# Sixteen starting places for the weight forms of the gate pairs and couples of a bidirectional trunk layer

## The chip, the cores and the metric

The kernel runs on one core of one Trainium2 chip, whose engines appear in the profile as PE (TensorE matmuls), PEld (TensorE weight loads, which overlap the matmuls), DVE (VectorE), ACT (ScalarE), POOL (GpSimd) and SP (SyncE, which issues most DMAs). The metric is the device time of one execution in microseconds, the median over several executions. A shorter time is better.

## The reference

One layer of an encoder on 512 positions of width 1024, all in float32. Only the matrix products matter here:

```python
proj = rmsnorm(x, g_pre_mix) @ w_in                  # q k v g u sv a_ret a_sgu
y_ret = (layernorm(retention(q, k, v)) * silu(g)) @ w_ret_o
y_sgu = (gelu(u) * spatial(layernorm(gelu(sv)))) @ w_sgu_o
x1 = x + rmsnorm((sigmoid(a_ret) * y_ret + sigmoid(a_sgu) * y_sgu) @ w_out, g_post_mix)
hid = conv3(rmsnorm(x1, g_pre_ffn) @ w_up)           # width 2 * 2816
y = x1 + rmsnorm((gelu(hid_a) * hid_b) @ w_down, g_post_ffn)
```

## The kernel before

**Precision.** Every float32 operand is split into a high and a low part of a faster float32 form (`split`, lines 83 to 85: ACT copies the high part, DVE subtracts it from the source and leaves the low part). A product is then three matmuls, high by high, high by low and low by high, accumulated in PSUM.

**Seven products for eight.** For some pairs of weight blocks the kernel doesn't use the weights as they are but seven sums of their quarters, called forms: B11, B21, T1, T2, T3, T4 and B22 (`FORMS`, line 91). `w_form` (lines 152 to 170) loads a pair of weight blocks, makes the sums on DVE and POOL, and splits each form into a tile `wf`: 512 columns of high part, then 512 columns of low part. `Pair` (from line 646) multiplies them. Its `product` (line 655) is twelve matmuls on line 662, four steps of three: the stationary operand is a slice of 128 columns of `wf`, the moving operand 256 columns of an activation (`xh` and `xl`, `h2h` and `h2l`) or of an activation form (`sh`, `sl`). A pair thus has 7 times 12, or 84 matmuls on line 662.

**Which pairs.** There are twenty: four for the column u of `w_in` (list places 32 to 39), eight for the gates a_ret and a_sgu (list places 40, 44, ... 68; `GATE0` is 40, `GATE1` is 72), and eight couples of the up projection (`COUPLES`, list places `UP0 + 2 * a` for a = 4, 6, ... 18, where `UP0` is 80). In a gate pair and in a couple the forms alternate with two whole weight blocks of 8 times three matmuls with 512 moving columns (`f_block`, lines 212 to 214).

**Where weights lie.** All weights of this kind come from one ring of nine slots (`slot`, lines 122 and 123). A slot has 1088 float32 elements, 4352 bytes or 17 times 256, so all nine start at the same place modulo 256 bytes. An argument `at` shifts the tile inside its slot by a number of elements: whole blocks start at 0 (at 48 in the down projection, line 138), weight forms at 16 (line 168), the weights of the down projection's own forms at 48 (line 188). A shift of 16 elements is 64 bytes. The activations are in blocks of 2048 bytes, and in the program their ring starts at the same place modulo 256 bytes as the ring of slots; a half of such a block (columns 256 to 511) starts 1024 bytes further, which is the same place again. So the distance modulo 256 bytes between the start of a stationary slice and the start of the moving operand is the tile's shift: 0 bytes for whole blocks, 64 bytes for forms. In the down projection the weights are the moving operand, at 192 bytes, and the activations the stationary one, at 0: 64 bytes again, counted in the same direction.

**Order.** Loads, splits and forms are issued ahead of their use by `w_get` (line 198), which keeps a fixed number of units in flight (`LOOK` is 4). The order on each engine is that of the program text. ACT, DVE and POOL prepare weights and activations while PE multiplies.

Of the kernel before, what the change touches and what calls it, by code (L numbers as in the profile page):

```python
# [27 lines left out]
U0, GATE0, GATE1 = 32, 40, 72  # L28
# [8 lines left out]
UP0 = DOWN0 - 2 * NF  # L37
COUPLES = [(i, i + 1) for i in range(4, 20, 2)]
# [8 lines left out]
def tile_block(ctx: ExitStack, tc, xT, x, wall, par, cs, wsp, bsp, gpost, gffn, out):  # L47
# [7 lines left out]
    def nm(s):  # L55
        uid[0] += 1
        return f"{s}_{uid[0]}"
# [25 lines left out]
    def split(hi, lo, src):  # L83
        copy(hi, src)
        nc.vector.tensor_sub(lo, src, as32(hi))  # L85
# [7 lines left out]
    i = 0  # L93
    while i < NW:
# [7 lines left out]
        elif i == UP0 + 2 * COUPLES[0][0]:  # L102
# [3 lines left out]
            i = UP0 + 2 * COUPLES[-1][1] + 2  # L106
# [12 lines left out]
    def raw_tile():  # L119
        return sb.tile([P, 1024], F32, tag="raw", bufs=4, name=nm("raw"))  # L120

    def slot(n, at=0, w=1024):
        return sb.tile([P, 1088], F32R, tag="w4", bufs=9, name=nm(n))[:, at : at + w]

    def w_block(i):
# [23 lines left out]
                split(hi, lo, raw)  # L149
        return hi, lo  # L150

    def w_form(form, i):

        if form == "B11":
            a, b = raw_tile(), raw_tile()
            nc.sync.dma_start(a, wall[i])
            nc.sync.dma_start(b, wall[i + 1])
            w_raw["B11"], w_raw["B12"] = a[:, :S], a[:, S:]
            w_raw["B22"], w_raw["B21"] = b[:, :S], b[:, S:]
        elif form == "T1":  # L160
            t = raw_tile()
            w_raw["T1"], w_raw["T2"], w_raw["T3"], w_raw["T4"] = t[:, :S], t[:, S:], w_raw["B12"], t[:, S:]
            nc.vector.tensor_add(w_raw["T1"], w_raw["B11"], w_raw["B12"])  # L163
            nc.vector.tensor_add(w_raw["T3"], w_raw["B12"], w_raw["B22"])
            nc.gpsimd.tensor_tensor(out=w_raw["T2"], in0=w_raw["T1"], in1=w_raw["B22"], op=ALU.add)  # L165
        elif form == "T4":
            nc.gpsimd.tensor_tensor(out=w_raw["T4"], in0=w_raw["T2"], in1=w_raw["B21"], op=ALU.add)
        w = slot("wf", 16)
        split(w[:, :S], w[:, S:], w_raw[form])
        return w[:, :S], w[:, S:]  # L170

# [20 lines left out]
    def w_unit(u):  # L192
        return w_block(u[1]) if u[0] == "blk" else (w_down if u[0] in "qt" else w_form)(*u)
# [4 lines left out]
    def w_get(look=LOOK):  # L198

        i = w_pos[0]  # L200
        w_pos[0] += 1
        room = 2 * look + (2 if w_size(units[i]) == 2 else 0)
        n = sum(w_size(u) for u in units[i : w_pos[1]])
        while w_pos[1] < len(units) and (w_pos[1] <= i or n + w_size(units[w_pos[1]]) <= max(room, 9 if look == LOOK else 0)):
            u = units[w_pos[1]]
            w_ready[w_pos[1]] = w_unit(u)
            w_pos[1] += 1
            n += w_size(u)
        return w_ready.pop(i)
# [768 lines left out]
    i = 0  # L978
# [83 lines left out]
    for j in range(DP):  # L1062
# [5 lines left out]
        if j in (3, 5):  # L1068
            w = w_get()
# [179 lines left out]
```

## Time and profile before

| | |
|---|---|
| median of three runs | 840.68 us (840.61 to 841.0) |
| the profiled execution | 839.4 us, of which the span of the profile is 837.6 us |
| mean granted TensorE clock | 0.994 |
| PE busy, instructions | 820.8 us (98%), 5152 |
| PEld busy | 738.7 us (88%) |
| DVE busy | 663.0 us (79%) |
| ACT busy | 429.7 us (51%) |
| POOL busy | 109.9 us (13%) |

The profile lists busy times by engine, a view of the span in slices, the chain of work that ended last, and groups of instructions by source line and by tiles. In a row such as `L662 PE MATMUL ps<-sh,wf` the tile written stands before the arrow and the tiles read behind it, with the buffer numbers left out. The end of a matmul is modelled, so the time of a single one overlaps the next; what it really takes in a stream is the distance between two starts. The view of the chain in order of time gives the start of a stretch, its length and, behind an x, how many instructions it merges.

### The profile page before, as it was taken

The numbers are of one execution on the slowest core, as the hardware profiler recorded it, in microseconds if no ns is written. First come the engines' busy times: TensorE is split into PE (matmuls) and PEld (weight loads), VectorE is DVE, ScalarE is ACT, GpSimd is POOL, SyncE is SP. The second block draws the span as 40 slices with busy tenths as digits, with TensorE's granted clock in tenths as the row PEclk, the third lists the DMA queues.
The fourth block names the chain that finished last, engine by engine and source line by source line (L and its number), as shares of the span: only waits on it lengthen the run. The fifth ranks groups of instructions, "written<-read, shape, count | busy, mean of one in ns | idle before, by whom it ended". The sixth has DMA issues, their size and how long they took to land.

```text
span 837.6 us, 13230 instructions
## 1 busy us (share of the span) xinstructions
PE 820.8 (98%) x5152; PEld 738.7 (88%) x5152; DVE 663.0 (79%) x1100; ACT 429.7 (51%) x729; POOL 109.9 (13%) x110
## 2 busy tenths in 40 slices
PE   9999999999999999999999999899999999999995
PEld 7888888888899999999988898799999998999995
DVE  7489888877897776877665669779799799988956
ACT  6635446545664533444444654456566566544531
POOL 0010000111221111122211224111111100000001
PEclk9999999999999999999999999999999999999998
DMA  8733212212233333333457120333333341233334
GB/s 286 246 114 111 76 66 76 75 51 101 88 101 102 101 101 101 101 99 103 136 161 283 65 63 26 101 101 101 101 101 101 101 151 51 76 117 123 114 126 152
DMA packets 29215, 93.24 MB, mean 111 GB/s; under 512 B 3360, under 2 KB 4000, under 8 KB 29152
## 3 DMA queue, kind: packets, MB, share of 16 engines
q1 hardware_dynamic: 26928, 86.85, 31.7%
q0 software_dynamic: 1360, 4.46, 1.6%
q10 hardware_dynamic: 864, 1.09, 0.4%
q8 instruction: 40, 0.66, 0.3%
q14 instruction: 23, 0.19, 0.1%
HBM read 88.19 MB, written 4.19 MB: 110 GB/s over the span
## 4 chain that ended last, share of the span: by engine, by line
PE 84%; DVE 10%; issue 2%; DMA 2%; ACT 1%; POOL 0%; DVEq 0%; POOLq 0%; ACTq 0%
PE ps L662 20%; PE ps L212 11%; PE ps L213 11%; PE ps L214 11%; PE ps L1017 6%; PE ps L473 5%; PE ps L474 5%; PE ps L475 5%; DVE wf L85 2%; PE ps L810 2%; PE ps L812 2%; PE ps L811 2%; DMA raw<-wall 2%; DVE dl L85 1%; PE ps L1033 1%
## 5 line engine op out<-in xcount | busy, mean ns | idle before, releaser
L85 DVE TENSOR_TENSOR wl<-raw,wh 128x1024 fp32r<-128x1024 f32 (+1 forms) x93 | 108.0, 1171 | 53.2 <-PE ps L662 29.1
L78 ACT ACTIVATE wf<-raw 128x512 fp32r<-128x512 f32 x140 | 84.4, 625 | 94.9 <-PE ps L213 45.8
L85 DVE TENSOR_TENSOR wf<-raw,wf 128x512 fp32r<-128x512 f32 x140 | 107.8, 785 | 26.9 <-ACT wf L78 25.9
L662 PE MATMUL ps<-sh,wf 128*128 128x256 f32 x640 | 123.3, 282 | 2.2 <-ACT sh L78 1.7
L78 ACT ACTIVATE wh<-raw 128x1024 fp32r<-128x1024 f32 (+2 forms) x95 | 93.1, 989 | 35.6 <-DMA raw<-wall 16.1
L662 PEld LDWEIGHTS ps<-sh,wf 128*128 128x128 f32 x640 | 102.2, 188 | 3.7 <-ACT sh L78 1.9
L212 PE MATMUL ps<-h2h,wh 128*128 128x512 f32 (+1 forms) x256 | 93.2, 366 | 0.0
L213 PE MATMUL ps<-h2l,wh 128*128 128x512 f32 (+1 forms) x256 | 93.2, 365 | 0.0
L214 PE MATMUL ps<-h2h,wl 128*128 128x512 f32 (+1 forms) x256 | 92.8, 363 | 0.0
L662 PE MATMUL ps<-sl,wf 128*128 128x256 f32 x320 | 90.0, 281 | 1.5 <-DVE sl L85 1.5
L473 PE MATMUL ps<-wh,xh 128*128 128x512 f32 x192 | 75.0, 391 | 0.0
L474 PE MATMUL ps<-wl,xh 128*128 128x512 f32 x192 | 74.9, 390 | 0.0
L475 PE MATMUL ps<-wh,xl 128*128 128x512 f32 x192 | 74.8, 390 | 0.0
L165 POOL TENSOR_TENSOR raw<-raw,raw 128x512 f32<-128x512 f32 x20 | 34.3, 1716 | 223.0 <-DVE raw L163 166.5
L662 PEld LDWEIGHTS ps<-sl,wf 128*128 128x128 f32 x320 | 61.3, 192 | 2.3 <-DVE sl L85 1.7
L1017 PE MATMUL ps<-dh,fh 128*128 128x256 f32 x216 | 60.1, 278 | 1.6 <-DVE e L1051 1.2
L1017 PE MATMUL ps<-dl,fh 128*128 128x256 f32 x216 | 60.0, 278 | 0.1
L1017 PE MATMUL ps<-dh,fl 128*128 128x256 f32 x216 | 59.9, 277 | 0.0
L214 PEld LDWEIGHTS ps<-h2h,wl 128*128 128x128 f32 x256 | 48.5, 190 | 7.8
L212 PEld LDWEIGHTS ps<-h2h,wh 128*128 128x128 f32 x256 | 48.4, 190 | 7.3 <-ACT h2h L878 0.3
L662 PE MATMUL ps<-xh,wf 128*128 128x256 f32 x288 | 54.7, 281 | 0.0
L213 PEld LDWEIGHTS ps<-h2l,wh 128*128 128x128 f32 x256 | 48.6, 190 | 6.6
(303 smaller groups left out, 2053.2 us busy)
## 6 DMA issues: line engine op xcount, KB each, us to landing
raw<-wall SPq DMA_DIRECT2D x145, 512.0 KB, 3.6
x<-x SPq DMA_DIRECT2D x24, 256.0 KB, 5.7
xT<-xT SPq DMA_DIRECT2D x8, 256.0 KB, 5.4
x<-x POOLq DMA_DIRECT2D x8, 256.0 KB, 2.3
xT<-xT POOLq DMA_DIRECT2D x4, 256.0 KB, 4.0
out<-zg SPq DMA_DIRECT2D x4, 256.0 KB, 2.1
out<-zs ACTq DMA_DIRECT2D x3, 256.0 KB, 3.8
cs<-cs SPq DMA_DIRECT2D x2, 256.0 KB, 4.2
```

The costliest lines, as they stand in the source:

```text
L78: nc.scalar.activation(out=o, in_=i, func=AF.Copy)
L85: nc.vector.tensor_sub(lo, src, as32(hi))
L165: nc.gpsimd.tensor_tensor(out=w_raw["T2"], in0=w_raw["T1"], in1=w_raw["B22"], op=ALU.add)
L212: nc.tensor.matmul(o, ah, bh, start=start, stop=False)
L213: nc.tensor.matmul(o, ah, bl, start=False, stop=False)
L214: nc.tensor.matmul(o, al, bh, start=False, stop=stop)
L473: nc.tensor.matmul(acc[t], xh[k][:, c], wh[:, f], start=k == 0, stop=False)
L474: nc.tensor.matmul(acc[t], xh[k][:, c], wl[:, f], start=False, stop=False)
L475: nc.tensor.matmul(acc[t], xl[k][:, c], wh[:, f], start=False, stop=k == KD - 1)
L662: nc.tensor.matmul(o, w_[:, c], a_, start=first and k == n == 0, stop=k == 3 and n == 2, skip_group_check=True,)
L810: nc.tensor.matmul(o, ah, bh, start=k == 0, stop=False)
L1017: nc.tensor.matmul(o, a_[:, c], w_[:, f], start=j == t == i == 0, stop=j == DP - 1 and i == 2 and n not in (M2, M3, M4), skip_group_check= ...
```

## The change

A function `place` gives the shift of a weight form inside its slot, where a constant 16 stood.

```diff
+    def place(i):
+
+        if i < GATE0:
+            return 16
+        return 2 * (i - GATE0) if i < GATE1 else 4 + 2 * (i - UP0 - 2 * COUPLES[0][0])
+
     def w_form(form, i):
...
-        w = slot("wf", 16)
+        w = slot("wf", place(i))
         split(w[:, :S], w[:, S:], w_raw[form])
```

The u pairs stay at 16 elements. The eight gate pairs get 0, 8, 16, ... 56 elements (0, 32, 64, ... 224 bytes), in the order of their use. The eight couples get 4, 12, 20, ... 60 elements (16, 48, 80, ... 240 bytes). The gate pair at list place 48 keeps its 16; the other fifteen pairs move. The last shift, 60, and the 1024 elements of a form still fit the slot's 1088. The list of instructions, their order on each engine and their waits are the same as before: the start addresses of 1260 matmul operands, 105 ACT and 105 DVE instructions differ, and nothing else.

## The prediction

> **What bounds the kernel now.** I read the page first: the engines' shares, the slices, the chain that ended last.
>
> ```profile
> span 837.6 us, 13230 instructions
> PE 820.8 (98%) x5152; PEld 738.7 (88%) x5152; DVE 663.0 (79%) x1100; ACT 429.7 (51%) x729; POOL 109.9 (13%) x110
> ...
> PE   9999999999999999999999999899999999999995
> ...
> PE 84%; DVE 10%; issue 2%; DMA 2%; ACT 1%; POOL 0%; DVEq 0%; POOLq 0%; ACTq 0%
> ```
>
> The matmul engine is busy in nearly every slice and is 84% of the chain. Next come the two stages in which the moved forms are used, the gates (262 to 430 us) and the couples (533 to 692 us): a view of busy time in these two stretches.
>
> ```profile
> core 0: us, PE busy (x) PEld busy (x) DVE busy (x) ACT busy (x) POOL busy (x), PEclk, DMA share, GB/s
> 262.00:430.00 168.00, 168.00 (x1072) 152.60 (x1071) 121.42 (x186) 73.94 (x124) 32.52 (x21) 1.00 0.33 107
> 533.00:692.00 159.00, 159.00 (x997) 143.82 (x996) 134.39 (x210) 91.69 (x156) 20.59 (x14) 0.99 0.32 103
> ```
>
> PE never rests there, at full granted clock but for the first microseconds of the couples. DVE has 46.6 and 24.6 us to spare, ACT 94.1 and 67.3. So only the pace from one matmul to the next can move the end. That pace is in the chain told in order of time, where a row gives start, length and the number merged.
>
> ```profile
> 388.29 5.65 PE ps L662 x48
> 393.94 0.23 PE ps L212
> ...
> 653.20 5.65 PE ps L662 x48
> ```
>
> Forty-eight form matmuls with 256 moving columns take 5.65 us, in the gates as in the couples: 117.7 ns each from these rounded rows. The x12 rows of line 662 below and others of 2.83 us for 24 give 117.9; I use 117.9. Here stationary and moving operand start 64 bytes apart modulo 256.
>
> Other rows of the same shape run at other paces. From the early up-projection blocks, one matmul to a row, and from the down projection:
>
> ```profile
> 399.41 1.41 PE ps L662 x12
> 403.57 2.83 PE ps L662 x24
> ...
> 480.27 0.12 PE ps L213
> ...
> 485.67 0.12 PE ps L213
> ...
> 752.09 5.44 PE ps L1033 x48
> ```
>
> Between the two rows of line 213 lie 45 matmuls (15 steps of three), so each takes 5.40/45 = 120.0 ns. These have 0 bytes between their operands. Line 1033, at 64 bytes again, takes 5.44/48 = 113.3. The three paces also show in the means of single matmuls, kept apart by shape, over the whole span:
>
> ```profile
> L662 PE MATMUL ps<-h2h,wf 128*128 128x256 f32 x192 | 36.5, 281 | 0.0
> ...
> L214 PE MATMUL ps<-h2h,wl 128*128 128x256 f32 x64 | 17.8, 283 | 0.0
> L1033 PE MATMUL ps<-wl,fh 128*128 128x256 f32 x64 | 17.7, 277 | 0.0
> ```
>
> A mean of 283 ns goes with 120.0, 281 with 117.9, 276 to 277 with 113.3. The first two rows are the cleanest pair in the trace: same moving tensor, same 256 columns, and the weights' place differs.
>
> But place is not all. The same groupings cut to stretches, first 236 to 256 us (u pairs), then 262 to 268 (first gate pair), then the down projection at 720 to 736 and at 780 to 815:
>
> ```profile
> L662 PE MATMUL ps<-sl,wf 128*128 128x256 f32 x33 | 9.1, 276 | 0.0
> ...
> L662 PE MATMUL ps<-sl,wf 128*128 128x256 f32 x3 | 0.8, 281 | 0.0
> ...
> L1017 PE MATMUL ps<-dl,fh 128*128 128x256 f32 x40 | 11.2, 281 | 0.0
> ...
> L1017 PE MATMUL ps<-dl,fh 128*128 128x256 f32 x89 | 24.6, 276 | 0.0
> ```
>
> At one and the same distance of 64 bytes a stream settles at 276 or at 281, and stays there for tens of microseconds. In the u pairs, where the fast one stands, the chain still runs over DVE and PE waits now and then:
>
> ```profile
> 242.59 1.58 DVE wf L85
> ```
>
> Where forms come straight after a 512-column block, as in every gate pair and couple, the trace shows 281.
>
> **The change part by part.** No instruction, wait, transfer or order changes; nothing is queued behind anything new. Addresses move on ACT, DVE and PE.
>
> *DVE and ACT.* 105 copies on ACT and 105 subtractions on DVE write the forms to other places. Two DVE lines show whether a shifted start costs: line 924 writes 511 elements from one element past the tile's start, line 928 writes 511 from the start itself.
>
> ```profile
> L924 DVE SCALAR_TENSOR_TENSOR cv<-ps,part,cv x28: 732/742/753, 494.4 to 717.6; 128x511 f32<-128x511 f32 x28
> ...
> L928 DVE SCALAR_TENSOR_TENSOR cv<-ps,part,cv x28: 735/744/752, 496.3 to 718.9; 128x511 f32<-128x511 f32 x28
> ```
>
> 742 against 744 ns (minimum, median, maximum stand in the rows): nothing. ACT has no such pair of rows; I take nothing as well, since its spare time, 94.1 + 67.3 us over 105 copies, would hide over 1 us for each. Should DVE pay after all, the cover is 46.6 + 24.6 us over 105 subtractions, or 0.68 us each, as much as one takes now (684 ns, first row below). Only at the start of the couples is that cover gone. There PE waits for activation forms that stand in DVE's queue among weight forms (second and third row), and its matmuls are slow for a while after it, 0.43 us where 512 columns take 0.23 (last row, from the chain):
>
> ```profile
> L85 DVE TENSOR_TENSOR wf<-raw,wf x140: 673/684/1825, 191.7 to 678.1; 128x512 fp32r<-128x512 f32 x140
> ...
> PE ps L662 <- ACT sh L78: 1.7, 1, 1.7
> PE ps L662 <- DVE sl L85: 1.5, 1, 1.5
> ...
> 532.76 0.43 PE ps L212
> ```
>
> About eight subtractions of the first couple stand ahead of these waits; at a tenth of 0.68 us more each that is 0.5 us. I count 0.
>
> *Matmuls.* Each of the fifteen moved pairs has 84 matmuls on line 662, so 1260 in all, 148.6 us of the span at 117.9 ns. This is the whole sum. One of the fifteen (the first gate pair) goes to 0 bytes, for which there is a row: 84 times (120.0 - 117.9) = +0.18 us. The other fourteen go to distances for which the trace has none. Bounds: downward 113.3 ns, the free pace, 1260 times -4.6 = -5.8 us. Upward 120.0 is the dearest row, 1260 times 2.1 = +2.6 us; and since nothing says that 0 bytes is the worst distance, I let half of the pairs pay a second step as large as that from 113.3 to 120.0, that is 126.7 ns, an estimate from those two rows: 630 times 2.1 plus 630 times 8.8 = +6.9 us.
>
> I take 120.0 for all. Two distances are known; after a 512-column block the 64 bytes start at 117.9 and the 0 bytes at 120.0, and no forms after such a block run at 113.3. The unknown ones are nearer to these two paces than to the free one.
>
> Sum on the profiled execution: 839.4 + 2.6 = 842.0 us (837.6 of it the span). That execution lies 1.3 us under the median of 840.68; on the median the sum is **843.3 us**, 0.3% slower.
>
> [...]
>
> **The rivals.**
>
> *Place does nothing here (chance 0.18).* The pace would be set by what came before the stream, as 276 and 281 at one distance show, and 283 would belong to the early blocks for another reason than their shift. Against it: at 0 bytes the 45 matmuls above never leave 120.0. Time: 840.7 us. The same time comes out if cheap and dear places cancel. [...]
>
> *The forms fall into the free pace (0.24).* At some distances the entry from a 512-column block may lead to 113.3, as a wait does at 64 bytes. For it: the free pace exists and, once reached, lasts through rows like the 48 of line 1033. If half of the moved matmuls reach it and half keep 117.9: 630 times -4.6 = -2.9 us, **837.8 us**. All of them: 834.9 us.
>
> *Some places are dearer than any row (0.16).* [...] Price as above, +6.9 us, **847.6 us**. It decides once the mean of the moved pairs is over 122 ns.
>
> *The forecast (0.42):* all near 120.0, 843.3 us.
>
> **How the numbers follow.** The 0.2% that a measurement of this kernel can tell from no change is 1.7 us, or 1.35 ns on each of 1260 matmuls. Faster is the free-pace rival, 0.24. Same is 0.18. Slower are the forecast and the dearer places, 0.42 + 0.16 = 0.58. The range goes from 837.8 (half of the free pace) to 847.6 us (the dearer places) and leaves out about a tenth on either side. The forecast's own range, with the mean of the moved pairs between 119.3 and 122 ns, is 842.4 to 845.8 us.
>
> **What would show it.** In the chain's rows for line 662 in the gates and couples, x48 goes from 5.65 to 5.76 us and x12 from 1.41 to 1.44; the single matmul's mean goes from 281 to 283. The first gate pair must show 120.0 and the gate pair left at 64 bytes 117.9; if the first doesn't, place isn't what sets the pace. Rows of 1.36 us for x12 would show the free pace, rows over 1.45 dearer places. Rows of the u pairs and of the down projection, and DVE's and ACT's durations for the forms, must stay. The prediction is wrong by its own reasons if PE's waits in the couples grow, or if the slow matmuls behind the waits at their start come to be more or fewer.

## The result and the profile after

The changed kernel takes 841.26 us (median of 20 executions, 839.86 to 843.54). Twenty executions of the kernel before, taken along with them, have a median of 839.81 us (838.0 to 841.41). The ratio is 1.0016, with a 95% interval from 1.0009 to 1.0023: slower by some 1.3 us. The forecast was slower by 2.6 us. The profiled execution took 841.5 us, 2.1 us more than the profiled one of before, and so did its span.

The page of the changed kernel: its span and the engines.

```profile
span 839.7 us, 13230 instructions
PE 823.1 (98%) x5152; PEld 741.0 (88%) x5152; DVE 663.9 (79%) x1100; ACT 430.0 (51%) x729; POOL 109.2 (13%) x110
```

The bound is still PE, 85% of the chain that ended last. Its busy time grew by 2.3 us with the same 5152 matmuls. The subtractions that write the forms (minimum, median, maximum in ns), and PE's waits at the start of the couples:

```profile
L85 DVE TENSOR_TENSOR wf<-raw,wf x140: 672/684/1825, 191.7 to 680.6; 128x512 fp32r<-128x512 f32 x140
...
PE ps L668 <- ACT sh L78: 1.9, 1, 1.9
PE ps L668 <- DVE sl L85: 1.5, 1, 1.5
```

The subtraction's median is 684 ns as before, that of ACT's copy 625 against 624, and the two waits are 1.9 and 1.5 us against 1.7 and 1.5. So DVE and ACT pay nothing for the shifted starts, and PE waits for nothing new. The two stages by their busy time (same columns as in the prediction):

```profile
262.00:430.00 168.00, 168.00 (x1073) 152.55 (x1072) 121.23 (x185) 73.16 (x122) 31.41 (x21) 1.00 0.33 107
533.00:692.00 159.00, 159.00 (x985) 143.64 (x985) 133.20 (x210) 90.55 (x155) 20.56 (x14) 0.99 0.32 103
```

PE never rests in either. What is left is the pace, and that is read from the chain told in order of time (start, length, number merged). Line 662 has become line 668. First the rows of before that give the starts of the same places in the program:

```profile
267.14 1.42 PE ps L662 x12
...
278.66 5.66 PE ps L662 x48
...
409.14 5.66 PE ps L662 x48
...
530.49 2.27 PE ps L662 x12
...
548.93 5.66 PE ps L662 x48
...
674.05 5.66 PE ps L662 x48
...
777.83 38.94 PE ps L1017 x341
```

Then the same view of the changed kernel. The first row is the u pairs, the next two the first gate pair (0 bytes). The x48 rows up to 410.61 are the gate pairs at 32, 64, 160 and 224 bytes, in this order; the two from 551.12 on are the couples at 48 and 240 bytes.

```profile
223.12 39.48 PE ps L668 x332
...
268.07 1.43 PE ps L668 x12
272.25 2.87 PE ps L668 x24
279.65 5.68 PE ps L668 x48
...
302.40 5.66 PE ps L668 x48
...
368.78 5.75 PE ps L668 x48
...
410.61 5.60 PE ps L668 x48
...
532.13 2.93 PE ps L668 x12
...
551.12 5.68 PE ps L668 x48
...
676.58 5.63 PE ps L668 x48
...
779.98 38.94 PE ps L1023 x341
```

Two things are to be seen. First, the pace now goes with the pair: 5.60 us (116.7 ns for one) at 224 bytes, 5.75 (119.8) at 112 and 160, the others between, 5.66 at the pair that did not move. The rows of 48 left out fit in: 5.70 at 96 and 128 bytes, 5.65 at 192, 5.69 at 80, 5.75 at 112 and 144, 5.67 at 176 and 5.60 at 208. Second, the starts tell where the 2.1 us arose:

| stretch | starts before, after | growth in it |
|---|---|---|
| up to the first gate pair's x12 row | 267.14, 268.07 | +0.93 |
| to the second gate pair | 278.66, 279.65 | +0.06 |
| second to eighth gate pair | 409.14, 410.61 | +0.48 |
| to the couples' first row | 530.49, 532.13 | +0.17 |
| first couple | 548.93, 551.12 | +0.55 |
| second to eighth couple | 674.05, 676.58 | +0.34 |
| to the long down-projection row | 777.83, 779.98 | -0.38 |

The stretches that hold the moved pairs grew by 0.48 + 0.34 us and a little in the first ones. The largest growth, 0.93 us, lies in the u pairs, which did not move, and in the first 48 matmuls of the first gate pair, which can account for some 0.1 us of it (48 times 2.1 ns). Another 0.55 us lies in the first couple: its first x12 row takes 2.93 us for 2.27, and behind it matmuls with 512 columns take 0.43 us where 0.23 is usual, in both kernels. The view of busy time tells why; first the kernel before, then the changed one (the granted clock PEclk is the third number from the end):

```profile
529.80:536.70 6.90, 6.49 (x28) 5.48 (x28) 6.87 (x12) 3.01 (x6) 0.00 (x0) 0.75 0.35 107
...
529.80:536.70 6.90, 5.37 (x19) 4.69 (x20) 6.90 (x12) 4.46 (x9) 0.00 (x0) 0.51 0.37 134
```

In these 6.9 us the mean granted clock is 0.75 before and 0.51 after. The twelve matmuls in 2.93 us take 244 ns each, twice the usual 117.9. So the slow start of the couples is a stretch of lower clock, and it lasted longer in this execution. The experiments show that both stretches, the u pairs and the start of the couples, vary by themselves.

### The profile page after: what moved, and what is told of

Same layout as the page of the kernel before. It is cut to its first block, busy times and chain, and to the rows that moved or that the text cites. A ratio compares the mean times of both kernels' runs of the same rounds, so it can differ in the third digit from the quotient of the medians.

```text
span 839.7 us, 13230 instructions
## 1 busy us (share of the span) xinstructions
PE 823.1 (98%) x5152; PEld 741.0 (88%) x5152; DVE 663.9 (79%) x1100; ACT 430.0 (51%) x729; POOL 109.2 (13%) x110
## 4 chain that ended last, share of the span: by engine, by line
PE 85%; DVE 8%; DMA 2%; issue 2%; ACT 1%; POOL 0%; DVEq 0%; POOLq 0%; ACTq 0%; SPq 0%
PE ps L668 23%; PE ps L218 11%; PE ps L219 11%; PE ps L220 11%; PE ps L479 5%; PE ps L480 5%; PE ps L481 5%; PE ps L1023 5%; DMA raw<-wall 2%; PE ps L818 2%; PE ps L816 2%; PE ps L817 2%; DVE dl L85 1%; PE ps L741 1%; DVE fl L85 1%
```

## The experiments

All kernels below are the changed kernel with the edit shown. Only `place`, a constant's width or the argument `at` of `slot` change; no kernel leaves work out. Ratios are against executions of the kernel before on the same chip; where one execution is named, there is one time and its profile.

**All sixteen pairs at 0 bytes.** The forecast priced all moved pairs by the 0-byte row, so this is its price measured by itself.

```diff
-        return 2 * (i - GATE0) if i < GATE1 else 4 + 2 * (i - UP0 - 2 * COUPLES[0][0])
+        return 0
```

> All gate pairs and couples start their forms at 0 bytes from the moving operand. Theory D (the distance of the two starts sets the pace): 120.0 ns per form matmul in every gate pair and couple, x48 rows of 5.74 to 5.76 us in the chain; 1344 matmuls times 2.1 ns = 2.8 us more than before, ratio 1.003. Theory P (a pair's neighbours in the program set its pace, not its place): x48 rows that differ from pair to pair as in the changed kernel, 5.60 to 5.75 us, ratio about 1.001.

Ratio 1.0038 (1.0023 to 1.0052), median 843.8 us. The chain, its last row of 48:

```profile
678.44 5.75 PE ps L668 x48
```

All fourteen rows of 48 are 5.75 or 5.76, in the gates and in the couples. The 0-byte row of the early blocks was read rightly: 0 bytes costs 119.8 ns wherever it is used. The position of a pair in the program has no part in it.

**All sixteen pairs at 208 bytes,** the cheapest place of the changed kernel's chain.

```diff
-        return 2 * (i - GATE0) if i < GATE1 else 4 + 2 * (i - UP0 - 2 * COUPLES[0][0])
+        return 52
```

> All gate pairs and couples start their forms at 208 bytes (52 elements), the place of the couple whose x48 row was 5.60 us. Theory D: 5.60 us in every x48 row, 116.7 ns per matmul, 1344 times -1.2 ns = -1.6 us, and the first 512-column matmuls behind each product recover sooner (18 ns, three times a pair: -0.9 us); sum -2.5 us, ratio 0.997. Theory P: x48 rows differ from pair to pair as in the changed kernel, ratio about 1.001.

Ratio 0.9976 (0.9966 to 0.9986), median 838.41 us: faster than both kernels, and the best that was measured here with an interval.

```profile
223.79 38.08 PE ps L668 x332
...
530.02 2.93 PE ps L668 x12
...
672.48 5.60 PE ps L668 x48
775.63 40.43 PE ps L1023 x341
```

Every pair shows 5.60 or 5.61. Added up, the rows of 12, 24 and 48 of gates and couples (1248 matmuls in each kernel) take 147.17 us before, 147.67 in the changed kernel, 149.33 at 0 bytes and 145.63 at 208 bytes: 117.9, 118.3, 119.7 and 116.7 ns for one. Now take the two rows whose code and places are those of the changed kernel: the u pairs take 38.08 us here and 39.48 there, and the long down row 40.43 for 38.94. So these stretches change by 1.4 and 1.5 us between executions with nothing changed in them. The slow start of the first couple (2.93) is here too, in a faster kernel. Over the ten runs whose chain has this row for u pairs at 64 bytes, it takes 38.08 to 38.35 us in six and 39.21 to 39.48 in four.

**The order of the places turned round,** so that each place is used by another pair, behind another pair.

```diff
-        return 2 * (i - GATE0) if i < GATE1 else 4 + 2 * (i - UP0 - 2 * COUPLES[0][0])
+        return 60 - 2 * (i - GATE0) if i < GATE1 else 56 - 2 * (i - UP0 - 2 * COUPLES[0][0])
```

> The same sixteen places, handed out otherwise: the gate pairs take 240, 208, ... 16 bytes, the couples 224, 192, ... 0. Theory D: each x48 row goes with its place. Gate pairs 2 to 8: 5.60, 5.67, 5.75, 5.75, 5.69, 5.68, 5.68 us; couples 2 to 8: 5.65, 5.75, 5.70, 5.70, 5.66, 5.68, 5.75 us. Theory P: the rows of the changed kernel in its order, gate pairs 2 to 8 5.68, 5.66, 5.70, 5.70, 5.75, 5.65, 5.60. In both the mean over the places is that of the changed kernel, so the ratio should repeat its 1.0016 within 0.001.

Ratio 1.0005 (0.9994 to 1.0016).

```profile
278.43 5.61 PE ps L668 x48
...
323.58 5.68 PE ps L668 x48
...
591.81 5.77 PE ps L668 x48
612.92 5.63 PE ps L668 x48
```

Eleven of fourteen rows of 48 are within 0.01 us of what the same place showed before: 5.61 at 208 bytes, which the second gate pair has now. (The changed kernel has no such row at 0 and 16 bytes; 0 is compared with the run before, 16 with what its rows of 12 and 24 give.) Three miss: 144 bytes 5.68 for 5.75, 128 bytes 5.77 for 5.70, and 96 bytes 5.63 for 5.70. The rows of 12 and 24 miss nowhere: at all sixteen places, these three included, both kernels agree within 0.01 us. So the place decides, but at 96, 128 and 144 bytes a row of 48 has two values, and the place alone does not choose between them. The forms add up to 147.80 us, 0.6 over the kernel before, as in the changed kernel (147.67); the ratio, expected at 1.0016 within 0.001, came out just below that.

**Everything moved by 64 bytes together,** stationary and moving operands alike, by a wider constant in front of both rings. The distances stay as in the changed kernel.

```diff
-    wact = const("wact", [P, 16])
+    wact = const("wact", [P, 32])[:, 0:16]
```

> The changed kernel, with a small tile at the front made 64 bytes wider, so that all activations and all weight slots start 64 bytes further and their distances stay. Theory D: pair by pair the x48 rows of the changed kernel, gate pairs 2 to 8 5.68, 5.66, 5.70, 5.70, 5.75, 5.65, 5.60 us. Theory A (the absolute place of the weights modulo 256 bytes sets the pace): the rows move up by two gate pairs, 5.70, 5.70, 5.75, 5.65, 5.60 us for pairs 2 to 6.

One execution, 839.49 us.

```profile
278.34 5.68 PE ps L668 x48
...
674.69 5.63 PE ps L668 x48
```

All fourteen x48 rows equal the changed kernel's, pair by pair. The absolute address falls as the cause, for a common shift of 64 bytes; the distance between the two operands stands. And this kernel, whose pairs have the changed kernel's paces, has a span of 837.7 us, 2.0 us under its: the span of one profile says less than the rows. Its granted clock from 529.8 to 536.7 us is 0.75, as in the kernel before.

**Steps of four bytes,** 176 to 204 bytes in the gates and 208 to 236 in the couples, to see the shape of the curve.

```diff
-        return 2 * (i - GATE0) if i < GATE1 else 4 + 2 * (i - UP0 - 2 * COUPLES[0][0])
+        return 44 + (i - GATE0) // 4 if i < GATE1 else 52 + (i - UP0 - 2 * COUPLES[0][0]) // 4
```

> The places go in steps of one element (4 bytes): gate pairs 176, 180, ... 204 bytes, couples 208, 212, ... 236. Theory D with a smooth map between the sixteen measured places: x48 rows of gate pairs 2 to 8 between 5.67 and 5.60 us, falling or level at 5.65 up to 192 bytes; couples 2 to 8 between 5.60 and 5.64. Rival L (only a place's 16-byte piece counts): rows equal in groups of four, 5.66, 5.65 and 5.60 us. Rival R (a start off a multiple of 16 bytes is dear): rows over 5.75 at three places of four.

One execution, 841.6 us, beside 838.41 us for one of the kernel before.

```profile
278.21 5.68 PE ps L668 x48
...
293.48 2.74 PE ps L668 x24
...
408.77 5.91 PE ps L668 x48
...
549.23 5.63 PE ps L668 x48
...
591.10 5.79 PE ps L668 x48
612.25 5.60 PE ps L668 x48
```

The first two rows are one pair, at 180 bytes; the others are 204, 212, 220 and 224 bytes. No theory held. The curve isn't smooth: 204 bytes takes 123.1 ns, more than any of the sixteen places, next to 208 bytes with 116.7. Nor is it level within 16 bytes: 212, 216 (5.74) and 220 bytes differ by up to 0.16 us. By rival L, for which only the 16-byte piece counts, 212, 216 and 220 bytes would show one pace; the rows show 5.63, 5.74 and 5.79 us. And the pair at 180 bytes has two paces: 118.3 ns in its row of 48, 114.2 in its row of 24, which is nearly the free pace of 113.3. So the free pace is not tied to 64 bytes.

**The u pairs at 208 bytes too.** This asks whether the free pace of 113.3 ns comes after any wait or belongs to a distance.

```diff
         if i < GATE0:
-            return 16
-        return 2 * (i - GATE0) if i < GATE1 else 4 + 2 * (i - UP0 - 2 * COUPLES[0][0])
+            return 52
+        return 52
```

> All twenty pairs, the u pairs too, at 208 bytes. Theory D: where the u pairs run without a wait they show 116.7 ns per matmul (9.8 us for 84) whatever went before, so a u stage between those of the two kept states at 64 bytes (9.52 and 9.89 us for 84). Rival F (the free pace after a wait belongs to every distance): after the waits in the first u pair the stream runs at 113.3 ns, modelled 276 ns, as at 64 bytes.

One execution, 837.77 us.

```profile
223.64 39.01 PE ps L668 x332
...
L668 PE MATMUL ps<-sl,wf 128*128 128x256 f32 x32 | 8.9, 278 | 0.0
```

The u pairs lie between their two values at 64 bytes (38.08 and 39.48). The mean of a single matmul, here from 236 to 256 us, is 278 ns, where 276 goes with the free pace. So behind the waits of the u pairs no free pace came at 208 bytes, and a stream at 64 bytes can be faster or slower than one at 208.

**The down projection at two distances.** There the weights are the moving operand.

```diff
-        hi, lo = slot("dh", 48, w), slot("dl", 48, w)
+        at = 12 if i < DOWN0 + DP + WHOLE // 2 else 52
+        hi, lo = slot("dh", at, w), slot("dl", at, w)
```

(with all sixteen gate pairs and couples at 208 bytes.)

> Gate pairs and couples at 208 bytes, and the down projection's own weights, which are the moving operand, at 12 elements in its first half and 52 in its second. Theory D, distance counted from the moving to the stationary start: first half at 208 bytes, 116.7 ns; second half at 48 bytes, 118.3 ns. Rival S (the sign doesn't count): first half at 48 bytes, 118.3; second half at 208, 116.7. Either way neither half is at 64 bytes, so the free 113.3 may be lost and the down projection take 112 to 114 us instead of about 111.

One execution, 837.93 us. The groups by shape, the first row from 720 to 736 us, the second from 780 to 815:

```profile
L1024 PE MATMUL ps<-dl,fh 128*128 128x256 f32 x35 | 9.8, 281 | 0.0
...
L1024 PE MATMUL ps<-dl,fh 128*128 128x256 f32 x85 | 24.0, 283 | 0.0
...
749.56 5.65 PE ps L1040 x48
```

The first half, at a distance of 208 bytes, shows a mean of 281 and not 278; the second, at 48 bytes, 283 and not 281. With the sign of the distance turned round the first half fits and the second, which should then show 278, does not. So in this execution the distances as measured on the forms do not give the pace of the down projection. Whether that comes from the place of the moving operand itself or from what runs in front isn't separated. The last row, from the chain, speaks for a part of the second: these are whole blocks that kept their 64 bytes, and they take 5.65 us where the kernel before has 5.44.

**The whole blocks at 208 bytes,** from the gates on, with all sixteen pairs at 208.

```diff
-            at = 48 if i >= DOWN0 else 0
+            at = 48 if i >= DOWN0 else 52 if i >= GATE0 else 0
```

> Gate pairs and couples at 208 bytes, and the whole blocks from the gates up to the down projection too. Theory D: the early up blocks with 256 moving columns go from 120.0 to 116.7 ns, 192 matmuls times -3.3 ns = -0.6 us; blocks with 512 columns keep 226.7 ns, since their weight load has twice the time; what changes there is only the first few behind a product. A rival in which the distance costs 512 columns as well would show it as another steady pace than 226.7.

One execution, 843.94 us. A group of 512-column matmuls in the gates:

```profile
L218 PE MATMUL ps<-yh,wh 128*128 128x512 f32 x64 | 25.3, 396 | 0.0
```

396 ns here, 391 before in the same group and stretch. I had expected that these stay. The longer time for a weight load (226.7 ns from start to start before, where the early blocks have 120.0) did not hold them. A gate pair grew from 20.72 us (408.48 - 387.76, the same two x48 starts with pairs at 208 and blocks at 0) to 21.00 (409.19 - 388.19). Of these two places, 0 bytes is the dear one for 256 columns and the cheap one for 512.

**Of the whole blocks only the early up-projection ones at 208 bytes,** with 256 columns, the rows from which the forecast took its 120.0; all sixteen pairs are at 208 too.

```diff
-            at = 48 if i >= DOWN0 else 0
+            at = 48 if i >= DOWN0 else 52 if UP0 <= i < UP0 + 4 else 0
```

> Gate pairs, couples and the four early up blocks (256 moving columns) at 208 bytes; everything else as before. Theory D: the kernel with pairs at 208 bytes came out at a ratio of 0.9976; the early blocks add 192 times -3.3 ns = -0.6 us, so 0.997 against before. A rival in which only forms from the pairs gain: 0.9976 again, early matmuls at 120.0 ns.

Ratio 0.9983 (0.9973 to 0.9992), median 838.37 us. The pairs keep 5.60 and 5.61. The early blocks, in the stretch from 470 to 500 us:

```profile
L220 PE MATMUL ps<-h2h,wl 128*128 128x256 f32 x64 | 17.5, 278 | 0.0
```

The mean of a single matmul is 278 ns where the kernel with the pairs alone at 208 bytes has 283 in the same group and stretch. 278 is the value of the forms at 208 bytes, so the place sets the pace here as well. As an addition to the pairs at 208 bytes its gain can't be told from none: the two intervals overlap.

**Forms at 64 bytes, the blocks between them at sixteen places.** This tests the entry: whether the pace of forms at one and the same distance depends on the block they follow.

```diff
+            if GATE0 <= i < GATE1:
+                at = 8 * ((i - GATE0) // 4)
+            elif UP0 + 2 * COUPLES[0][0] <= i < UP0 + 2 * COUPLES[-1][1] + 2:
+                at = 4 + 8 * ((i - UP0 - 2 * COUPLES[0][0]) // 4)
...
+        return 16
```

> Forms stay at 64 bytes everywhere, and the two whole blocks of each gate pair and couple go to sixteen places, 0, 32, ... 224 bytes in the gates and 16, 48, ... 240 in the couples. Theory D for 512 columns: 226.7 ns at 0, 232 to 233 at 208 bytes, other paces at other places. Theory E (what stands before a stream decides which of the two paces it falls into at 64 bytes): the forms, at one place all through, run at 113.3 ns behind blocks at some places and at 117.9 behind others; x48 rows of 5.44 beside 5.66 us. If E is wrong, all x48 rows stay at 5.66.

One execution, 840.18 us. Line 668 is now 672.

```profile
317.70 2.73 PE ps L672 x24
...
325.00 5.46 PE ps L672 x48
...
347.72 5.66 PE ps L672 x48
...
389.42 5.45 PE ps L672 x48
...
409.96 5.46 PE ps L672 x48
...
544.43 2.83 PE ps L672 x24
550.06 5.46 PE ps L672 x48
```

All of these are forms at 64 bytes. The x48 row comes behind the last block of the pair ahead (at the second to fifth gate pair with sixteen small matmuls between), the x24 row behind a block of its own pair. Behind blocks at 32 bytes the row is 5.66; behind 64 bytes it is 2.73 and then 5.46 (113.8 ns); behind 96 bytes 5.66; behind 160 and 192 bytes 5.45 and 5.46. So one distance has two paces, and what stands in front has a part in the choice. The block's place alone does not choose: in the couples the rows of 24 behind blocks at 16 and 208 bytes take 2.83 us, the slow pace, and the rows of 48 behind blocks at the same places 5.46 and 5.45, the free one. The price stands at the blocks: most of them are slower than at 0 bytes, with means of 393 to 395 ns by group in the gates against 389 to 391 before. The best gate pair takes 20.54 us (409.96 - 389.42) against 20.85 before (409.14 - 388.29).

**All blocks at 192 bytes, forms at 64.** If the block's place alone chose after all, every pair would take the 20.54 us.

```diff
+            if GATE0 <= i < GATE1 or UP0 + 2 * COUPLES[0][0] <= i < UP0 + 2 * COUPLES[-1][1] + 2:
+                at = 48
+            elif UP0 <= i < UP0 + 4:
+                at = 52
...
+        return 16
```

> Forms at 64 bytes as before; the whole blocks of gate pairs and couples at 192 bytes, the four early up blocks at 208. Theory E: behind blocks at 192 bytes all forms run at 113.3 ns as in the seventh gate pair of the block scan, where the blocks took 229 ns a matmul instead of 226.7; that pair was 0.32 us shorter than before, so 15 to 16 pairs give -5 us, and the early blocks -0.6 us: 834 us, ratio 0.9935, x48 rows of 5.44 us. Rival (that pair's state came from the pairs ahead of it, not from its blocks): x48 rows of 5.66 and, with the dearer blocks, no gain, ratio 1.000 to 1.001.

Ratio 0.9999 (0.9977 to 1.002). The twelve times go from 834.94 to 845.37 us, three times as wide as those of the kernel before beside it (838.0 to 841.57). The profiled execution is the slowest, 845.37 us.

```profile
L222 PE MATMUL ps<-gh,wh 128*128 128x512 f32 x64 | 25.4, 397 | 0.0
```

In it all fourteen rows of 48 are 5.65 or 5.66, none free, and the blocks are at 397 ns, the slowest in this study. A gate pair takes 21.11 us (411.62 - 390.51). So the place of the block isn't enough either. That the executions near 835 us are those in which the free pace was reached is likely, but no profile of one was taken.

**Blocks at 192 bytes, forms at 208.** The same blocks, with the forms at the place that had one pace so far.

```diff
+        return 52
```

> As the kernel before it in this call, with the forms of gate pairs and couples at 208 bytes instead of 64. If the free 113.3 ns belongs to 64 bytes alone, x48 rows are 5.60 us as with blocks at 0, and the dearer blocks make it 2 us longer than blocks at 0 with forms at 208 bytes. If any distance can reach the free pace behind such blocks, x48 rows are 5.44.

One execution, 840.8 us.

```profile
L222 PE MATMUL ps<-yh,wh 128*128 128x512 f32 x64 | 25.2, 393 | 0.0
```

The forms show 5.60 or 5.61 throughout: behind blocks at 192 bytes as behind blocks at 0, 208 bytes shows one pace. The blocks at 192 bytes are at 393 here and at 397 in the run above, so they have more than one pace too. A pair takes 20.82 us (409.01 - 388.19), 0.10 more than with blocks at 0.

## Why the prediction was right in its sign and wrong in its size

**What bounds the kernel: right.** Only the pace of PE moved. DVE's 684 ns stayed and ACT's copy went from 624 to 625, so the zero for DVE and ACT stood.

**"One of the fifteen (the first gate pair) goes to 0 bytes, for which there is a row": right.** The first gate pair shows 1.43 for 12 and 2.87 for 24, 119.4 ns for one of these 36, and the run with all pairs at 0 bytes has 119.8 in every pair. The gate pair that kept its 64 bytes stayed at 5.66.

**"I take 120.0 for all" is the step that failed,** a term of the sum that was too large. I had two distances that follow a 512-column block, 0 and 64 bytes, took the dearer for the fourteen unknown ones, and gave as reason that they are nearer to these two than to the free pace. That they were: 116.7 to 119.8 in the rows of 48, up to 120.4 in a row of 24 (2.89 us at 128 bytes). But 0 bytes is close to the top of the sixteen places, and 208 and 224 bytes lie under both. Without the unmoved pair (9.91 us for 84), the moved ones take 137.76 us for 1164 matmuls in the rows of the chain, 118.4 ns. The term 1260 times 2.1 ns (+2.6 us) measured 1260 times 0.5 ns (+0.6 us) in the forms themselves. The starts of the pairs, which hold the blocks between the forms as well, give 0.8 us. The middle of the two known rows, 118.95 ns, would have given +1.3 us and been nearer; the rows gave no reason to prefer an end. The sign came out as forecast, but by a small balance of cheap and dear places: all pairs at 208 bytes are 1.5 us below the kernel before in these rows and all at 0 bytes 2.2 above, and which places lie below 64 bytes was not foreseen. In so far the sign was luck.

**The rest of the measured 1.3 us.** The interval of the ratio, 0.8 to 1.9 us, just reaches the 0.8. Whether something else in the changed kernel adds to it, or the medians of two sets of executions with wandering stretches differ by chance, these runs don't settle. Two things on record bear on it. The same sixteen places in the other order, with the same sum of the forms, gave 1.0005. And the time goes with the mean granted clock of an execution: the changed kernel's eight executions at 0.994 took 839.86 to 841.12 us, its twelve at 0.991 to 0.993 took 841.02 to 843.54. The clocks of the 20 executions of the kernel before that were taken along are not on record, so what part of the 1.3 us the clock has stays open. The 2.1 us between the two profiles are mostly such wandering: +0.93 in the u pairs up to the first gate pair, +0.55 at the start of the couples, where the clock was 0.51 and not 0.75, and -0.38 before the long down-projection row. The forecast demanded that the rows of the u pairs and of the down projection stay. The u pairs did not stay (281 ns for 276 from 236 to 256 us), and this was no effect of the change: with the same code they took 38.08 us in one run and 39.48 in another.

**The rivals.** "Place does nothing" is refuted by 5.60 against 5.75 us for 48 in one execution (116.7 and 119.8 ns for one), by the places turned round, and by the two runs with all pairs at one place: 0.0062 of the time lies between their ratios. That cheap and dear places cancel, which I had put with this rival, is nearly what happened in the forms. "The forms fall into the free pace" did not come about: no moved pair has a row under 5.60. But its mechanism is real, as the rows of 5.46 behind blocks at 64, 160 and 192 bytes and the 2.74 for 24 at 180 bytes show. "Some places are dearer than any row" did not come about either: the mean of 118.4 is far from the 122 that it asked for. A place of that kind exists at 204 bytes (5.91), which is not among the sixteen.

**"If the slow matmuls behind the waits at their start come to be more or fewer".** They became more (2.93 for 2.27), and the longer of PE's waits there went from 1.7 to 1.9 us. The slow matmuls are those under the lower clock, from 529.8 to 536.7 us 0.51 on the mean where the kernel before has 0.75. With both operands moved by 64 bytes, the same distances as in the changed kernel and the same rows of 48, the clock in that stretch is 0.75 as before, and the first couple takes 18.48 us (549.23 - 530.75) where the kernel before has 18.44 and the changed one 18.99; so the 0.51 is not tied to the places; each is one execution.

## What to carry to other kernels

Where PE never rests, the start of the stationary operand against that of the moving one, modulo 256 bytes, is worth measuring: the edit is one constant, the places of the changed kernel gave from 116.7 to 119.8 ns for a matmul in the rows of 48, and 208 bytes for the forms took 0.24% (0.14 to 0.34) off an already tuned kernel. Measure the exact place with the exact shape and the exact neighbours: a matmul at 204 bytes took 5% longer than at 208 (123.1 and 116.7 ns), 208 bytes, with 224 the cheapest of the sixteen places with 256 columns, is worse than 0 with 512 (means of 396 and 391 ns), and forms at 64 bytes took 5.66 us for 48 behind blocks at 96 bytes and 5.46 behind blocks at 192. Compare rows of the chain for the pairs themselves, not spans, since stretches elsewhere move by more than the effect from one execution to the next: the same u pairs took 38.08 or 39.48 us, while the forms of the changed kernel grew by some 0.6 us.

## What the hardware showed that I had not expected

- A matmul of 256 columns in a stream takes from 113.3 to 123.1 ns here (5.44 and 5.91 us for 48), by the places of its operands and by what ran before, with the same data and no wait.
- The pace is the same if both operands move by 64 bytes (fourteen rows of fourteen), is not smooth at steps of 4 bytes, and is not a function of the distance alone: in the down projection, with the moving operand shifted by 48 or 208 bytes, one execution showed 281 and 283 ns where 278 and 281 were expected.
- Matmuls of 512 columns have paces of their own: means of 391 ns at 0 bytes, 396 at 208 bytes, and 393 or 397 at 192 bytes.
- At 64 bytes a stream has two paces (5.45 or 5.46 against 5.66 us for 48 forms), and the u pairs kept one from 236 to 256 us (means of 276 to 278 ns before, 281 in the changed kernel): one and the same code took 38.08 or 39.48 us. At 180 bytes there are two as well (118.3 and 114.2 ns). A kernel that leans on this (blocks at 192 bytes) spreads over 10.4 us. What makes these paces, no run here shows.
